# Gates as columns, spread by DMA, and merged products ahead of the short ones in a two-layer decoder trunk

## The chip, the core and the metric

The kernel runs on one core of one Trainium2 chip. A core has a matmul engine (TensorE, PE in the profile; its weight loads are PEld), a vector engine (VectorE, DVE), a scalar engine (ScalarE, ACT), a general engine (GpSimd, POOL) and an engine that only issues transfers (SyncE, SP). They work side by side and meet through semaphores. Transfers (DMAs) run on 16 DMA engines that all queues share; POOL, ACT and SP each have a queue for issuing them. The on-chip memory SBUF has 128 partitions; matmuls write to PSUM, eight banks of 512 floats per partition.

The metric is the device time of one execution, in microseconds, as the median over runs.

## The reference

256 tokens of width 1024 go through two layers. Each layer adds three branches to the running x: a SwiGLU feed-forward (hidden width 2816), an attention (block-sparse in layer 0, latent attention with a shared K/V in layer 1) and a second feed-forward. All data are 32-bit floats.

Every branch is modulated by a condition vector c. From `silu(c) @ ada_w + ada_b` come, per branch, a shift, a scale and a gate, each 1024 wide:

```python
mods = c_act @ ada_w[layer] + ada_b[layer]
sh1, sc1, g1, sh2, sc2, g2, sh3, sc3, g3 = jnp.split(mods, 9, axis=-1)
h = modulate(rms_norm(x, norm_g[layer, 0]), sh1, sc1)
x = x + 0.5 * g1[:, None, :] * swiglu(h, w_gate, w_up, w_down)
```

There are six gates (three branches in each of two layers). A gate multiplies the branch's output column by column, so all 256 rows see the same 1024 numbers. Shift and scale act on the normalised x in the same way.

## The kernel before

**Layout.** The 256 tokens are two tiles of 128. A branch's input h is held transposed (width on partitions, tokens along the row), so shift and scale are one number per partition there: a column. The branch's output has tokens on partitions and width along the row, so a gate has to be a row of 1024 numbers repeated on all 128 partitions: the tile `gate`.

**Products at full precision from rounded parts.** A weight tile is split by `split` (L643, L644) into a high part (a rounded copy on ACT) and a low part (what is left, on DVE); activations likewise. A product of two floats is high x high, high x low and low x high, accumulated in PSUM. In attention and in the down projection `mm3` (L773 to L775) issues these three, each over up to 512 columns. In the gate-and-up part of a feed-forward the weight is the stationary side, and the activations' high and low parts lie side by side (2 x 256 columns). There one *merged* product (L970, 512 columns) multiplies the weight's high part by both, and one *short* product (L977, 256 columns) multiplies the weight's low part by the activations' high part. The short one adds to the second half of the merged one's PSUM bank; ACT (L981) and DVE (L982) then sum the halves, L984 and L985 make `silu(gate) * up`, and L788 and L789 split the result for the down projection.

**The feed-forward's loops.** A block is 256 columns of the hidden width, with two weight tiles of 1 MB (one of w_gate, one of w_up), each split in two pieces of 1024 columns. It holds two steps of 128 hidden columns. In a step there are two parts, first "gate", then "up", and for each part the source issues eight merged products (over the 1024 input rows), then eight short ones, and then the evacuation of its PSUM bank. There are 35 blocks: 8 in the first feed-forward, 9 in each of the others, whose first 512 columns go through `mm3`. Then come the down projection, the residual (`resid`, L883, which multiplies by `gate`) and the next branch's norm, whose reciprocal root is a power on POOL (L810). The heads' norms in attention use POOL as well (L1138).

**The modulation vectors.** Their weights are streamed as 160 tiles of 512 KB. For shift and scale the weights are stored transposed: one DVE instruction (`column`, L654) multiplies a tile by the condition, which `c_b` repeats on all partitions, and sums along the row, which gives one column of 128 numbers, bias included. The read of its accumulator stands as a second small record on the same line. For a gate the weights are stored as they come: `ada_gate` adds eight tiles, each times the condition's column `cact`, into `acc` (L692, on DVE). POOL has filled `acc` with zeros (L690) and loaded the bias into its row 0 (L691). The sum over `acc`'s 128 partitions is still to be made: `acc` is split (a high part on ACT, a low part on DVE), two products by a matrix of ones (L702, L703) for each half of 512 columns sum it and repeat the sum on all partitions at once, in a PSUM buffer with a name of its own (`adaps`), and ACT copies it to `gate` with the factor 0.5 or 1 (L705).

**What sets the order.** The source is written against a rough clock of PE's work (`pe(us)`, `later(us, fn)`): `ada_pace` spreads the modulation tiles over a stage, `later` puts a piece of work behind so much PE work. After that the class `Order` plans anew: it takes all instructions with their dependences, an estimated duration for each (`duration`) and the buffer rings of every pool, and places them engine by engine, POOL's queue of transfers included; what it decides is written down as the fixed order of each engine. On PE it prefers, among what is ready, the instruction that comes first in the source; products into `adaps` go ahead of all others, or wait up to 3 us for their turn. On the other engines it takes the one that is needed soonest. The tiles of the last gate, (1, 2), are held until the last feed-forward has begun (`late`).

**Buffers that the change touches.** `ps_mm` has four PSUM banks for products (`mm_tile`), `ps_tr` three for transposes and scores (`tr_tile`), `ps_ada` one. `modp` has two gate tiles. `rawp` has three weight tiles, `splitp` eight high and eight low pieces.

Of the kernel before, what the change touches and what calls it, by code (L numbers as in the profile page):

```python
# [21 lines left out]
P = 128  # L22
D = 1024
# [47 lines left out]
NORMS = [(0, 0), (0, 1), (0, 2), (1, 0), (1, 1), (1, 2), "kv"]  # L71
NK = KD * len(NORMS)


# [52 lines left out]
def lay_out(v):  # L127
# [12 lines left out]
    out["first"] = out["first"].reshape(KD, P, 3, -1).transpose(0, 2, 1, 3)  # L140
    mats, cols, rows = [], np.zeros((P, 3, NK), np.float32), []
    for key, i in vectors():
        w, b, c = ((v["kv_ada_w"], v["kv_ada_b"], i) if key == "kv" else
                   (v["ada_w"][key[0]], v["ada_b"][key[0]], 3 * key[1] + i))
        w, b = w[:, c * D:(c + 1) * D], b[c * D:(c + 1) * D]
        mats.append((w if i == 2 else w.T).reshape(KD, P, D))
        if i == 2:
            rows.append(b)
        else:
            c0 = NORMS.index(key) * KD  # L150
            cols[:, i, c0:c0 + KD] = b.reshape(KD, P).T
    gains = np.concatenate([v["norm_g"].reshape(6 * KD, P), v["kv_norm_g"].reshape(KD, P)])
    cols[:, 2] = gains.T
    pos = np.ascontiguousarray(v["positions"].reshape(S))
    more = [v["c"].reshape(KD, P).T, pos.view(np.float32).reshape(NT, P).T]
    for n in ("moba_q_g", "moba_k_g"):
        more.append(np.tile(v[n][0], 2)[:, None])
    for g in (v["mla_q_g"][0], v["mla_k_g"]):
        more += [np.concatenate([g[:DH], np.ones(P - DH, np.float32)])[:, None], np.tile(g[None, DH:], (P, 1))]
    out.update(ada=np.stack(mats), rows=np.stack(rows), cols=np.concatenate([cols.reshape(P, -1), *more], axis=1))  # L160

# [376 lines left out]
def trunk(ctx: ExitStack, tc: tile.TileContext, a: dict, out: bass.AP):  # L538
# [88 lines left out]

    all_cols = cp.tile([P, 3 * NK + KD + NT + 4 + 2 * RO], F32, name="cols")
    places = {}
    c0 = 3 * NK  # L630
    for name, n in (("c", KD), ("pos", NT), ("moba_q", 1), ("moba_k", 1), ("q", 1), ("q_pe", RO), ("k", 1), ("k_pe", RO)):
        places[name] = all_cols[:, c0:c0 + n]
        c0 += n
    cols, cact = all_cols[:, :3 * NK].rearrange("p (i c) -> p i c", i=3), places["c"]
    m_cols = cp.tile([P, 2, NK], F32, name="m_cols")

# [36 lines left out]
    def ada_cols(j, key, i):  # L673
# [8 lines left out]
        yield  # L682

    def ada_gate(j, key, row):

        for k in range(KD):
            with noted(late if key == (1, 2) else set()):
                if k == 0:
                    acc = adap.tile([P, D], F32, tag="acc", name=nm("acc"), bufs=1)
                    nc.gpsimd.memset(acc, 0.0)  # L690
                    nc.gpsimd.dma_start(acc[0:1, :], a["rows"][row:row + 1, :])  # L691
                nc.vector.scalar_tensor_tensor(acc, ada_tile(j, k), cact[:, k:k + 1], acc, op0=ALU.mult, op1=ALU.add)  # L692
            if k < KD - 1:
                yield
        ahi, alo = split(acc, D)
        t = mods[key, "g"] = modp.tile([P, D], F32, tag="gate", name=nm("gate"))

        def sums():
            for hh in range(2):
                pt = ps_ada.tile([P, 512], F32, tag="ada", name=nm("adaps"))  # L700
                sl = slice(hh * 512, (hh + 1) * 512)
                nc.tensor.matmul(pt, ones_r, ahi[:, sl], start=True, stop=False)  # L702
                nc.tensor.matmul(pt, ones_r, alo[:, sl], start=False, stop=True)  # L703
                pe(0.44)
                nc.scalar.activation(t[:, sl], pt, AF.Copy, scale=1.0 if key[1] == 1 else 0.5)  # L705
            ready.add((key, "g"))
        later(3.0, sums)
        yield
# [185 lines left out]
    def ffn(layer, idx, h, after, ada_to, start=None):  # L894

        last = (layer, idx) == (1, 1)
        with ExitStack() as st:
# [50 lines left out]
            for f0 in range(B1 * P if start else FB, F, S):  # L948
# [9 lines left out]
                for f in range(f0 // P, (f0 + S) // P):  # L958
                    j = (f - f0 // P) % n
                    if not j:  # L960
                        both = (tp.tile([P, 512], F32, tag="ry", name=nm("ry"), bufs=1) if start else
                                sumsp.tile([P, 1024], F32, tag="both", name=nm("both")))
                        both = both.rearrange("p (i n t q) -> p i n t q", i=2, t=NT, q=P)
                    for i, pl in enumerate(parts):
                        ps = mm_tile()
                        for k in range(KD):
                            if len(pl) <= k:
                                pl += nextw()
                            wh = pl[k][0][:, f * P - f0:(f + 1) * P - f0]
                            nc.tensor.matmul(ps, wh, hk_both(h, k).rearrange("p i t q -> p (i t q)"),  # L970
                                             start=k == 0, stop=False)
                            pe(0.227)
                            if start and k in HOOKS and f0 < SIDE_TO * S:
                                bias_step()
                        for k in range(KD):
                            wl = pl[k][1][:, f * P - f0:(f + 1) * P - f0]
                            nc.tensor.matmul(ps[:, S:], wl, hk_both(h, k)[:, 0].rearrange("p t q -> p (t q)"),  # L977
                                             start=False, stop=k == KD - 1)
                            pe(0.12)
# [536 lines left out]
    def first(units):  # L1516
# [5 lines left out]
        with ExitStack() as st:  # L1522
# [30 lines left out]
            with ranked(0):  # L1553
                nc.scalar.activation(c_b[0:1, :], c_b[0:1, :], AF.Silu)
                for i in range(2):
# [3 lines left out]
                    nc.scalar.activation(c_b[:, half], pt, AF.Copy)  # L1559
                nc.scalar.activation(cact, cact, AF.Silu)  # L1560
            ps_x = [tr_tile(), ps_ada.tile([P, 512], F32, tag="ada", name=nm("tr"))]
# [113 lines left out]
```

## Time and profile before

| | us |
|---|---|
| median of three runs | 996.17 |
| lowest and highest run | 995.87, 996.71 |
| the profiled execution | 995.87 |
| its span, from first to last instruction | 994.1 |
| PE busy | 979.9 (99%) |
| DVE busy | 844.2 (85%) |
| ACT busy | 615.5 (62%) |
| POOL busy | 77.7 (8%) |

The profile's page gives the busy time of each engine, the costliest groups of instructions, and a chain of waits followed back from the last instruction. A row of a group reads: source line, engine, operation, what it writes and reads, count, then busy time in us, mean ns of one, and the idle time of the engine before them with what ended it. A row of the timeline or of the chain reads: start, duration, what. Matmuls are pipelined: the record of one with 512 columns lasts 0.39 us, while the next starts before it ends, so the cost of one is read from the distance of starts.

The stages lie as follows, by the timeline: the first feed-forward to about 208 us, the block-sparse attention to 330, the second feed-forward to 520, the third to 700, the latent attention to 805, the last feed-forward to the end.

### The profile page before, as it was taken

To read this page: it belongs to the slowest core of one execution; us is meant where nothing else is said; L and a number is where in the kernel's file an instruction comes from. 1 tells how busy PE (TensorE), PEld (TensorE's weight loads), DVE (VectorE), ACT (ScalarE), POOL (GpSimd) and SP (SyncE) were. 2 spreads that over 40 slices of the span, in tenths; PEclk is the share of its full clock that TensorE was granted. 3 is DMA by queue.
4 is the path that set the end of the run, shared out by engine and by line. 5 is a ranking of instruction groups with operands and counts; after the bars stand their busy time and mean duration, and the time that the engine had idled before them with its cause. 6 is when DMAs were issued, how large, how long until landed. Compare 5 with 4: busy or idle time off the path is not lost.

```text
span 994.1 us, 15134 instructions
## 1 busy us (share of the span) xinstructions
PE 979.9 (99%) x5558; PEld 831.1 (84%) x5558; DVE 844.2 (85%) x1391; ACT 615.5 (62%) x1113; POOL 77.7 (8%) x120
## 2 busy tenths in 40 slices
PE   9999999999999999999999999999989999999998
PEld 6988888878887888888888888888878888888886
DVE  7999999799999999999799999844998789667542
ACT  5689665378756965555377555643879685557421
POOL 2011000022221000000000000000052010000000
PEclk9999999999999999999999999999999999999999
DMA  9979889798887789988888999552343467444630
GB/s 353 403 289 304 333 292 358 299 339 333 284 313 246 267 326 330 326 299 310 340 332 330 340 320 327 208 195 88 106 154 128 170 253 287 180 170 175 227 127 21
DMA packets 54235, 260.51 MB, mean 262 GB/s; under 512 B 6289, under 2 KB 6801, under 8 KB 35986
## 3 DMA queue, kind: packets, MB, share of 16 engines
q1 hardware_dynamic: 52850, 256.06, 70.4%
q0 software_dynamic: 1024, 3.17, 1.1%
q8 instruction: 43, 0.70, 0.3%
q10 hardware_dynamic: 288, 0.33, 0.1%
q14 instruction: 30, 0.25, 0.1%
HBM read 255.34 MB, written 4.19 MB: 261 GB/s over the span
## 4 chain that ended last, share of the span: by engine, by line
PE 73%; DVE 10%; issue 10%; DMA 4%; ACT 2%; POOL 1%; SPq 0%; DVEq 0%; ACTq 0%; POOLq 0%
PE mm L970 21%; PE mm L773 12%; PE mm L775 12%; PE mm L774 12%; PE mm L977 11%; DVE lo L644 3%; DMA raw<-in_w_dram 2%; PE at L1101 1%; PE at L1078 1%; DMA adaw<-in_ada_dram 1%; PE tr L823 1%; DVE oh L1221 1%; DMA raw<-in_first_dram 1%; ACT hi L643 1%; DVE acc L692 1%
## 5 line engine op out<-in xcount | busy, mean ns | idle before, releaser
L644 DVE TENSOR_TENSOR lo<-raw,hi 128x1024 fp32r<-128x1024 f32 (+3 forms) x312 | 371.3, 1202 | 90.1 <-ACT hi L643 69.6
L643 ACT ACTIVATE hi<-raw 128x1024 fp32r<-128x1024 f32 (+3 forms) x312 | 315.8, 1038 | 157.9 <-PE mm L775 115.8
L970 PE MATMUL mm<-h,hi 128*128 128x512 f32 x1120 | 288.7, 394 | 0.8 <-ACT hi L643 0.8
L970 PEld LDWEIGHTS mm<-h,hi 128*128 128x128 f32 x1120 | 199.8, 189 | 36.0 <-ACT hi L643 1.0
L977 PEld LDWEIGHTS mm<-h,lo 128*128 128x128 f32 x1120 | 155.2, 190 | 11.9
L977 PE MATMUL mm<-h,lo 128*128 128x256 f32 x1120 | 162.1, 283 | 0.0
L654 DVE CUSTOM_DVE_ANT_0 adaw<-adaw,c_b,cols 128x1024 f32<-128x1024 f32 x112 | 141.8, 1279 | 1.9 <-DMA adaw<-in_ada_dram 1.9
L773 PE MATMUL mm<-hi,gh 128*128 128x512 f32 x352 | 137.3, 390 | 0.0
L775 PE MATMUL mm<-hi,gl 128*128 128x512 f32 x352 | 137.1, 389 | 0.0
L774 PE MATMUL mm<-lo,gh 128*128 128x512 f32 x352 | 137.0, 389 | 0.0
L981 ACT ACTIVATE both<-mm 128x256 f32<-128x256 f32 x108 | 40.5, 376 | 90.2 <-PE mm L977 89.8
L773 PE MATMUL mm<-hi,h 128*128 128x512 f32 (+1 forms) x240 | 94.5, 400 | 0.5 <-ACT h L788 0.5
L775 PE MATMUL mm<-hi,h 128*128 128x512 f32 (+1 forms) x240 | 92.4, 391 | 1.4 <-DVE h L789 1.4
L774 PE MATMUL mm<-lo,h 128*128 128x512 f32 (+1 forms) x240 | 93.3, 393 | 0.0
L775 PEld LDWEIGHTS mm<-hi,gl 128*128 128x128 f32 x352 | 66.1, 188 | 13.7
L774 PEld LDWEIGHTS mm<-lo,gh 128*128 128x128 f32 x352 | 66.1, 188 | 13.5
L773 PEld LDWEIGHTS mm<-hi,gh 128*128 128x128 f32 x352 | 66.1, 188 | 13.4
L692 DVE SCALAR_TENSOR_TENSOR acc<-adaw,cols,acc 128x1024 f32<-128x1024 f32 x48 | 61.5, 1282 | 0.1
L982 DVE TENSOR_TENSOR both<-both,mm 128x256 f32<-128x256 f32 x108 | 44.9, 416 | 12.0 <-ACT both L981 11.6
L775 PEld LDWEIGHTS mm<-hi,h 128*128 128x128 f32 x240 | 45.0, 188 | 10.3 <-DVE h L789 1.7
L773 PEld LDWEIGHTS mm<-hi,h 128*128 128x128 f32 x240 | 45.1, 188 | 10.1 <-issue 1.2
L774 PEld LDWEIGHTS mm<-lo,h 128*128 128x128 f32 x240 | 45.1, 188 | 7.7
(234 smaller groups left out, 1173.8 us busy)
## 6 DMA issues: line engine op xcount, KB each, us to landing
raw<-in_w_dram SPq DMA_DIRECT2D x142, 1024.0 KB, 6.0
adaw<-in_ada_dram SPq DMA_DIRECT2D x160, 512.0 KB, 5.7
raw<-in_first_dram SPq DMA_DIRECT2D x24, 256.0 KB, 7.5
raw<-in_w_dram SPq DMA_DIRECT2D x12, 512.0 KB, 3.6
raw<-in_w_dram SPq DMA_DIRECT2D x6, 576.0 KB, 3.7
bias_d<-bt SPq DMA_DIRECT2D x12, 256.0 KB, 5.8
bg<-bias_d POOLq DMA_DIRECT2D x4, 768.0 KB, 8.2
raw<-in_w_dram SPq DMA_DIRECT2D x2, 768.0 KB, 4.1
```

The source lines that it names most:

```text
L643: nc.scalar.activation(hi, src, AF.Copy)
L644: nc.vector.tensor_tensor(lo, src, hi.bitcast(F32), op=ALU.subtract)
L654: nc.vector.tensor_tensor_reduce(wt, wt, c_b, 1.0, cols[:, i, c:c + 1], op0=ALU.mult, op1=ALU.add, accum_out=m_cols[:, i, c:c + 1])
L692: nc.vector.scalar_tensor_tensor(acc, ada_tile(j, k), cact[:, k:k + 1], acc, op0=ALU.mult, op1=ALU.add)
L773: nc.tensor.matmul(ps, lh, rh, start=start, stop=False)
L774: nc.tensor.matmul(ps, lh, rl, start=False, stop=False)
L775: nc.tensor.matmul(ps, ll, rh, start=False, stop=stop)
L823: nc.tensor.transpose(kslice(pt, j), kslice(y, j), ident)
L970: nc.tensor.matmul(ps, wh, hk_both(h, k).rearrange("p i t q -> p (i t q)"), start=k == 0, stop=False)
L977: nc.tensor.matmul(ps[:, S:], wl, hk_both(h, k)[:, 0].rearrange("p t q -> p (t q)"), start=False, stop=k == KD - 1)
L981: nc.scalar.activation(sums, ps[:, S:], AF.Copy)
L982: nc.vector.tensor_tensor(sums, sums, ps[:, :S], op=ALU.add)
```

## The change

Two parts.

**Gates.** The weights of the gates are now stored transposed as well. `ada_gate` makes a gate like a shift: one multiply-and-sum on DVE per tile gives a column of 128 numbers with the bias, eight columns per gate, in `g_cols`. PE transposes the 128x8 columns to 8x128 in one of the `tr` banks, ACT copies them (factor 0.5 or 1) to `g_row`, POOL's queue stores these 4 KB in a tile in HBM, `gate_d`, and a second transfer on POOL's queue reads them back as one row of 1024 numbers, repeated on all 128 partitions, into `gate`. `acc` with its fill, its bias load, its split, the products by ones and the evictions of `adaps` go, and so do the condition as a column (`cact`) and its SiLU at the start. The biases of the gates travel in the packed columns.

**The feed-forward's order.** In a step, the merged products of "gate" and of "up" come first, then the short ones of "gate" with its evacuation, then the short ones of "up" with its evacuation. Both PSUM banks of the step are asked for ahead of the products.

```diff
-        mats.append((w if i == 2 else w.T).reshape(KD, P, D))
+        mats.append(w.T.reshape(KD, P, D))
         if i == 2:
-            rows.append(b)
+            gates.append(b.reshape(KD, P).T)
...
-    more = [v["c"].reshape(KD, P).T, pos.view(np.float32).reshape(NT, P).T]
+    more = [*gates, pos.view(np.float32).reshape(NT, P).T]
...
-    all_cols = cp.tile([P, 3 * NK + KD + NT + 4 + 2 * RO], F32, name="cols")
+    all_cols = cp.tile([P, 3 * NK + NGATE * KD + NT + 4 + 2 * RO], F32, name="cols")
...
+    gate_d = dp.tile([NGATE, KD, P], F32, name="gate_d")
+    g_cols = cp.tile([P, NGATE, KD], F32, name="g_cols")
+
     def ada_gate(j, key, row):
 
         for k in range(KD):
             with noted(late if key == (1, 2) else set()):
-                if k == 0:
-                    acc = adap.tile([P, D], F32, tag="acc", name=nm("acc"), bufs=1)
-                    nc.gpsimd.memset(acc, 0.0)
-                    nc.gpsimd.dma_start(acc[0:1, :], a["rows"][row:row + 1, :])
-                nc.vector.scalar_tensor_tensor(acc, ada_tile(j, k), cact[:, k:k + 1], acc, op0=ALU.mult, op1=ALU.add)
+                wt, c = ada_tile(j, k), row * KD + k
+                nc.vector.tensor_tensor_reduce(wt, wt, c_b, 1.0, places["gates"][:, c:c + 1], op0=ALU.mult, op1=ALU.add,
+                                               accum_out=g_cols[:, row, k:k + 1])
             if k < KD - 1:
                 yield
-        ahi, alo = split(acc, D)
         t = mods[key, "g"] = modp.tile([P, D], F32, tag="gate", name=nm("gate"))
 
-        def sums():
-            for hh in range(2):
-                pt = ps_ada.tile([P, 512], F32, tag="ada", name=nm("adaps"))
-                sl = slice(hh * 512, (hh + 1) * 512)
-                nc.tensor.matmul(pt, ones_r, ahi[:, sl], start=True, stop=False)
-                nc.tensor.matmul(pt, ones_r, alo[:, sl], start=False, stop=True)
-                pe(0.44)
-                nc.scalar.activation(t[:, sl], pt, AF.Copy, scale=1.0 if key[1] == 1 else 0.5)
+        def spread():
+            pt = tr_tile()
+            nc.tensor.transpose(pt[:KD, :P], g_cols[:, row], ident)
+            pe(0.11)
+            g_row = sp.tile([KD, P], F32, tag="grow", name=nm("grow"), bufs=1)
+            nc.scalar.activation(g_row, pt[:KD, :P], AF.Copy, scale=1.0 if key[1] == 1 else 0.5)
+            nc.gpsimd.dma_start(gate_d[row], g_row)
+            nc.gpsimd.dma_start(t, bcast_row(gate_d[row], D))
             ready.add((key, "g"))
-        later(3.0, sums)
+        later(3.0, spread)
...
-                    for i, pl in enumerate(parts):
-                        ps = mm_tile()
+                    pss = [mm_tile() for _ in parts]
+                    for ps, pl in zip(pss, parts):
                         for k in range(KD):
                             if len(pl) <= k:
                                 pl += nextw()
...
+                    for i, (ps, pl) in enumerate(zip(pss, parts)):
                         for k in range(KD):
                             wl = pl[k][1][:, f * P - f0:(f + 1) * P - f0]
                             nc.tensor.matmul(ps[:, S:], wl, hk_both(h, k)[:, 0].rearrange("p t q -> p (t q)"),
...
-                nc.scalar.activation(cact, cact, AF.Silu)
```

More of the change, by code (lines that the diff above doesn't have):

```diff
@@ L72 @@
 NK = KD * len(NORMS)
+NGATE = len(NORMS) - 1
 def vectors():
@@ L140, in lay_out @@
     out["first"] = out["first"].reshape(KD, P, 3, -1).transpose(0, 2, 1, 3)
-    mats, cols, rows = [], np.zeros((P, 3, NK), np.float32), []
+    mats, cols, gates = [], np.zeros((P, 3, NK), np.float32), []
     for key, i in vectors():
@@ L159, in lay_out @@
         more += [np.concatenate([g[:DH], np.ones(P - DH, np.float32)])[:, None], np.tile(g[None, DH:], (P, 1))]
-    out.update(ada=np.stack(mats), rows=np.stack(rows), cols=np.concatenate([cols.reshape(P, -1), *more], axis=1))
+    out.update(ada=np.stack(mats), cols=np.concatenate([cols.reshape(P, -1), *more], axis=1))
     table = np.concatenate([np.zeros((1, H), np.float32), v["rel_bias"]])
@@ L626, in trunk @@
     pos_f = a["positions"].rearrange("o s -> (o s)")
-    all_cols = cp.tile([P, 3 * NK + KD + NT + 4 + 2 * RO], F32, name="cols")
+    all_cols = cp.tile([P, 3 * NK + NGATE * KD + NT + 4 + 2 * RO], F32, name="cols")
     places = {}
     c0 = 3 * NK
-    for name, n in (("c", KD), ("pos", NT), ("moba_q", 1), ("moba_k", 1), ("q", 1), ("q_pe", RO), ("k", 1), ("k_pe", RO)):
+    for name, n in (("gates", NGATE * KD), ("pos", NT), ("moba_q", 1), ("moba_k", 1), ("q", 1), ("q_pe", RO), ("k", 1), ("k_pe", RO)):
         places[name] = all_cols[:, c0:c0 + n]
         c0 += n
-    cols, cact = all_cols[:, :3 * NK].rearrange("p (i c) -> p i c", i=3), places["c"]
+    cols = all_cols[:, :3 * NK].rearrange("p (i c) -> p i c", i=3)
     m_cols = cp.tile([P, 2, NK], F32, name="m_cols")
```

## The prediction, made before the changed kernel was run

> **What bounds the kernel now.** I read the page first: busy shares, then the chain of work that ended last.
>
> ```profile
> span 994.1 us, 15134 instructions
> ...
> PE 979.9 (99%) x5558; PEld 831.1 (84%) x5558; DVE 844.2 (85%) x1391; ACT 615.5 (62%) x1113; POOL 77.7 (8%) x120
> ...
> PE 73%; DVE 10%; issue 10%; DMA 4%; ACT 2%; POOL 1%; SPq 0%; DVEq 0%; ACTq 0%; POOLq 0%
> ```
>
> The matmul engine is busy 99% of the span and carries 73% of the chain. A busy PE could still be a slow one, so I next read busy times by stage (columns: PE, weight loads, DVE, ACT, POOL, then clock, DMA share, GB/s).
>
> ```profile
> 50.00:90.00 40.00, 39.23 (x461) 33.34 (x460) 39.87 (x102) 37.06 (x82) 6.35 (x37) 1.00 0.82 292
> 90.00:152.00 62.00, 61.97 (x351) 54.04 (x351) 61.21 (x110) 41.15 (x75) 4.32 (x5) 1.00 0.88 315
> 208.00:330.00 122.00, 121.51 (x682) 97.56 (x681) 115.88 (x224) 89.26 (x189) 26.24 (x17) 1.00 0.82 294
> 352.00:454.00 102.00, 102.00 (x585) 89.46 (x584) 98.06 (x136) 61.41 (x95) 2.98 (x4) 1.00 0.90 324
> 695.00:805.00 110.00, 104.96 (x657) 89.33 (x656) 96.43 (x225) 87.36 (x220) 26.24 (x25) 1.00 0.40 137
> ```
>
> In the gate-and-up part of a feed-forward (352 to 454) PE has no gap at all; in the first one (50 to 152) DVE is just as full (39.87 of 40.00, 61.21 of 62.00). The last question is what one matmul costs in the stream. The chain of waits inside that part, and a row from each end of a steady run of 512-column products (20 starts, 199.79 to 204.09), give it:
>
> ```profile
> 376.94 0.95 PE mm L977 x8
> 377.89 1.84 PE mm L970 x8
> ```
> ```profile
> 199.79 0.39 PE L773 MATMUL mm<-hi,gh 128*128 128x512 f32 x1
> ...
> 204.09 0.39 PE L774 MATMUL mm<-lo,gh 128*128 128x512 f32 x1
> ```
>
> A merged product (512 columns) costs 1.84 / 8 = 0.230 us, a short one (256 columns) 0.95 / 8 = 0.119 us, whatever the 0.39 us that a record lasts. So PE sets the end, and a matmul taken out of its queue is worth its 0.23 us wherever PE has no gap around it.
>
> **The gates: what goes.** Per gate four products over 512 columns of ones leave PE, with two evictions and a split on ACT, a split on DVE, and a fill and a small load on Pool.
>
> ```profile
> L654 DVE CUSTOM_DVE_ANT_0 adaw<-adaw,c_b,cols 128x1024 f32<-128x1024 f32 x112 | 141.8, 1279 | 1.9 <-DMA adaw<-in_ada_dram 1.9
> ...
> L692 DVE SCALAR_TENSOR_TENSOR acc<-adaw,cols,acc 128x1024 f32<-128x1024 f32 x48 | 61.5, 1282 | 0.1
> ...
> L654 DVE DVE_READ_ACCUMULATOR2_ANT m_cols<- 128x1 f32 x112 | 9.2, 82 | 0.0
> ...
> L644 DVE TENSOR_TENSOR lo<-acc,hi 128x1024 fp32r<-128x1024 f32 x6 | 7.3, 1224 | 1.9 <-PE mm L977 1.8
> L705 ACT ACTIVATE gate<-adaps 128x512 f32<-128x512 f32 x12 | 7.1, 594 | 2.4 <-PE adaps L703 2.2
> ...
> L643 ACT ACTIVATE hi<-acc 128x1024 fp32r<-128x1024 f32 x6 | 6.4, 1062 | 2.6 <-PE mm L970 1.6 <-PE mm L775 1.0
> ...
> L702 PE MATMUL adaps<-hi,ones_r 128*128 128x512 f32 x12 | 4.8, 401 | 0.0
> ...
> L703 PE MATMUL adaps<-lo,ones_r 128*128 128x512 f32 x12 | 4.7, 396 | 0.0
> ```
>
> PE: 12 products at L702 and 12 at L703, 24 x 0.230 = 5.5 us less, all on the path. ACT loses 6.4 + 7.1 = 13.5 us and DVE 7.3 us of splits; both are cover, priced at nothing of their own since PE has no gap there to close. The 48 products of a weight tile with the condition stay on DVE under another instruction, 1.279 us against 1.282 us: no change. (Its accumulator read adds at most 48 x 0.082 = 3.9 us to DVE, less than the 7.3 us that go.) Six fills and six loads leave Pool, which is 8% busy.
>
> **The gates: what comes.** Per gate one transpose on PE, a small copy on ACT (the 128x512 eviction takes 0.59 us; an 8x128 one not more), and on Pool's queue a 4 KB store and a 512 KB load that spreads the row. The trace has transposes in the stream of products only in pairs:
>
> ```profile
> 212.01 0.38 PE L823 MATMUL tr<-ident,y 128*128 128x128 f32 x2
> 212.15 0.48 PE L773 MATMUL mm<-hi,h 128*128 128x512 f32 x1
> 212.46 0.39 PE L773 MATMUL mm<-hi,gh 128*128 128x512 f32 x1
> ```
>
> From 212.01 to 212.46 pass 0.45 us for a pair and one product; less 0.23, a pair costs 0.22 us. A single one costs between 0.11 (half) and 0.22 (if the switch, not the second tile, is the price); I take 0.12, since a second transpose only adds its own stream. Six: 0.7 us, at most 1.3. (Each now borrows one of the three transpose buffers for its copy instead of a buffer of its own; at most 0.59 us six times, and the third buffer covers it.) The gates' sum on PE is -5.5 + 0.7 = -4.8 us, -4.2 at the dear end.
>
> The two transfers follow one another, since the second reads what the first stored. Their nearest rows are the small loads on the same queue and the bias loads (768 KB):
>
> ```profile
> L691 POOL DMA_DIRECT2D acc<-in_rows_dram x6: 501/547/669, 2.5 to 799.6; - x6
> ...
> DMA to landing us min/median/max: 1.7/3.6/5.7
> ```
> ```profile
> bg<-bias_d POOLq DMA_DIRECT2D x4, 768.0 KB, 8.2
> ```
>
> By the medians a gate is 3.6 + 8.2 = 12 us later than its transpose, by the worst store 5.7 + 8.2 = 14 us. The tightest gate is the first: its last eviction starts at 133.60, and the residual that reads it at 182.55.
>
> ```profile
> 133.60 0.60 ACT L705 ACTIVATE gate<-adaps 128x512 f32<-128x512 f32 x1
> ```
> ```profile
> 182.55 0.68 DVE L883 TENSOR_TENSOR ry<-mm,gate 128x512 f32<-128x512 f32 x1
> ```
>
> That is 48 us of cover for 14, so the latency costs nothing; without cover it would be 14 us a gate. The page DMA: Bandwidth & Descriptors of the Trainium skill (section "Anatomy of one DMA") gives 2.0 us plus bytes over 436 GB/s per transfer on this path, as an estimate 2.0 + 3.2 = 5.2 us for the two; by either the cover holds.
>
> ```profile
> cols<-in_cols_dram SPq DMA_DIRECT2D x1, 123.0 KB, 2.2
> ```
>
> At the start, one SiLU of eight columns on ACT goes, and the packed columns grow by 40 floats a partition (3 x 56 + 48 + 70 = 286 for 246); 20 KB beside weights at 292 GB/s and more is 0.07 us. I count neither.
>
> **The feed-forward's order.** The 35 blocks hold 140 runs of eight merged products and 140 of eight short ones; afterwards two runs of a kind follow each other, so about 70 changes of length each way go. Eight steady 512-column products cost 8 x (204.09 - 199.79) / 19 = 1.81 us; after short ones eight cost 1.84. So a change costs 0.03 us, of which the short side gives some 0.01 back: 70 x 0.02 = 1.4 us, between 0 (if the 0.03 belongs to the operands' places, not to the change) and 2.1. I take 1.2.
>
> The second half of each pair ("up") is wanted 0.95 us earlier in its split's high part, and the low part of "gate" 1.84 us later. Where the high part is late, PE waits. One such wait stands at the first block:
>
> ```profile
> 51.34 2.00 PE L970 MATMUL mm<-h,hi 128*128 128x512 f32 x8
> 53.18 1.11 PE L977 MATMUL mm<-h,lo 128*128 128x256 f32 x8
> 55.06 1.20 PE L970 MATMUL mm<-h,hi 128*128 128x512 f32 x4 [0.77 <-ACT hi L643]
> ```
> ```profile
> L970 PE MATMUL mm<-h,hi 128*128 128x512 f32 x1120 | 288.7, 394 | 0.8 <-ACT hi L643 0.8
> ```
>
> There the short products would follow instead of precede, and the block ends when it did. The group of all 1120 merged products has 0.8 us of idle time, which is this one, so elsewhere the splits run ahead. The two accumulators of a pair are held together, but the four PSUM buffers turn over in two pairs of 5.58 us (2 x 2.79), and an evacuation needs about 1: no wait. The evacuations move with the short products: that of "gate" comes 1.84 us later, just ahead of that of "up", and what follows (sum, SiLU, split) still has the next pair's 5.58 us.
>
> **Sum.** -4.8 - 1.2 = -6.0 us. The profiled execution took 995.87 us around its span of 994.1; 995.87 - 6.0 = 989.9, and against the median of 996.17, 990.2 us. Its own bounds: -4.2 - 0 gives 992.0, and -4.8 - 2.1 gives 989.3.
>
> **Rivals.**
> *Gates alone.* The source only proposes PE's order; the planner in the kernel places each instruction, and may interleave the runs anyway. Then -4.8: 991.4. Against it: in the rows at 376.94 its order is the source's.
> *More than the sum.* Net of the accumulator reads DVE loses some 3.5 us, most of it in stages where it is full. If all of that closes gaps of PE (994.1 - 979.9 = 14.2 us of them), 986.7. The full stages hold little of them (40 - 39.23, 122 - 121.51), so little supports it.
> *Given back.* The new plan makes "up" wait for its high split. If one block of six loses 0.95 us, 35 / 6 x 0.95 = 5.5 us return: 995.7. For it: DVE and ACT orders are planned anew everywhere; against: the 0.8 us of idle time above.
> *Pool's queue held.* The spreading load waits on Pool for the store to land, and what stands behind it there waits too. At the change from feed-forward to attention this is the norm's power:
>
> ```profile
> 208.06 1.47 POOL L810 TENSOR_TENSOR rstd<-ssq,mhalf 128x1 f32<-128x1 f32 x1 [85.09 <-DVE ssq L805]
> ...
> 215.91 1.07 POOL L1253 DMA_DIRECT2D bg<-bias_d  x1 [4.64 <-PE mm L775]
> 219.57 1.47 POOL L810 TENSOR_TENSOR rstd<-ssq,mhalf 128x1 f32<-128x1 f32 x1 [2.60 <-DVE ssq L805]
> ```
>
> A second gate transposed near 207 and a load issued just ahead of 219.57 cost 0.55 + 5.7 + 1.07 = 7.3 us at worst: 990.2 + 7.3 = 997.5. Against: the planner holds the load back until it reckons the store landed, and 11 us lie between the two powers. The page SBUF — State Buffer of the Trainium skill (section "Who interferes with whom") warns that DVE copies in their two-port mode lock Pool out while it writes descriptors, some 0.6 us becoming 3.1; the L691 row, 0.50 to 0.67 us beside a DVE at 85%, does not show it.
> *Slower: the spreading loads push the weights.* Six times 512 KB at 315 GB/s are 6 x 1.67 = 10.0 us of transfer time in stages whose DMA share is 0.82 to 0.90. If the weights have no reserve, PE waits all of it: 990.2 + 10.0 = 1000.2. The sign turns where a load holds PE up by 1.0 us. The waits speak against it:
>
> ```profile
> ACT hi L643 <- PE mm L775: 116.8, 77, 9.1
> ...
> ACT hi L643 <- DMA raw<-in_w_dram: 9.2, 7, 1.9
> ```
>
> The splits wait for buffers that PE frees (116.8 us), seldom for weights (9.2).
>
> **How the numbers follow.** Forecast 0.50, gates alone 0.16, more than the sum 0.08, given back 0.12, Pool's queue 0.06, weights pushed 0.08. A measurement of this kernel tells about 0.2% (2 us) from no change: the first three are faster (0.74), given back and Pool's queue same (0.18), the last slower (0.08). The range 987.0 to 996.5 leaves out the last two and part of "more".
>
> **What would show it.** No L702 and L703, six transposes, DVE's lo<-acc gone; merged products in runs of 16 near 3.65 us and short ones near 1.91; the spreading loads landing within 14 us, tens of us ahead of L883; idle time of the merged products still near 1 us. Wrong would make it: that idle time at several us, the norm's power late with a load ahead of it, or splits waiting on weights for clearly more than 9.2 us.

## The result, and the profile after

The changed kernel takes 990.18 us (median of six runs, 989.76 to 990.75); the kernel before, run beside it, 996.02 (995.33 to 996.76). The ratio is 0.9938, with an interval of 0.9927 to 0.9949: 5.8 us faster, where 990.2 was predicted. The profiled execution took 989.81 us.

The first lines of the page, and its chain by engine, of the changed kernel:

```profile
span 988.0 us, 15123 instructions
...
PE 975.1 (99%) x5540; PEld 829.4 (84%) x5540; DVE 834.3 (84%) x1433; ACT 606.0 (61%) x1100; POOL 76.9 (8%) x120
...
PE 89%; DVE 6%; DMA 2%; ACT 1%; issue 1%; POOL 0%; SPq 0%; DVEq 0%; ACTq 0%
```

The span is 6.1 us shorter, PE is as full as before, and PE now carries 89% of the chain. DVE is busy for 9.9 us less and ACT for 9.5.

The chain of waits inside the second feed-forward of the changed kernel (start, us, what) shows the new order of products:

```profile
376.84 1.91 PE mm L979 x16
378.76 3.65 PE mm L971 x16
382.41 1.91 PE mm L979 x16
```

Sixteen merged products take 3.65 us, sixteen short ones 1.91. Before, the same 32 products took 2 x (1.84 + 0.95) = 5.58 us, now 5.56. That is 0.02 us for the one change of length each way that went. Over all undisturbed steps of the two traces the medians are 5.587 and 5.567 us, so the 0.02 is not a matter of rounding.

A gate's transpose among merged products, by the timeline of PE in the changed kernel:

```profile
356.21 0.86 PE L971 MATMUL mm<-h,hi 128*128 128x512 f32 x3
356.91 0.27 PE L701 MATMUL tr<-ident,g_cols 128*8 128x128 f32 x1
356.94 1.39 PE L971 MATMUL mm<-h,hi 128*128 128x512 f32 x5
```

The next product starts 0.03 us after the transpose. Its group of five lasts 1.39 us, of which the last product's record is 0.39: 1.00 us from the first start to the fifth, where four steady distances are 4 x 0.227 = 0.91. So the transpose costs 0.03 + 0.09 = 0.12 us, paid by the product behind it. By the starts, all six transposes of the trace come out at 0.11 to 0.12 us.

The groups by line in the changed kernel (busy us, mean ns | idle before):

```profile
L971 PE MATMUL mm<-h,hi 128*128 128x512 f32 x1120 | 270.3, 392 | 0.6 <-ACT hi L644 0.6
...
L693 DVE CUSTOM_DVE_ANT_0 adaw<-adaw,c_b,cols 128x1024 f32<-128x1024 f32 x48 | 60.7, 1276 | 0.0
...
L693 DVE DVE_READ_ACCUMULATOR2_ANT g_cols<- 128x1 f32 x48 | 3.8, 80 | 0.0
```

No new idle time stands before the merged products: 0.6 us, against 0.8.

The two transfers of a gate, by the landings of lines L705 and L706 of the changed kernel (4 KB store, then the 512 KB spread), and the first reading of a spread gate on DVE:

```profile
L705 POOL DMA_DIRECT2D gate_d<-grow x6: 522/570/697, 128.1 to 894.6; - x6
...
DMA to landing us min/median/max: 4.1/4.7/5.5
```
```profile
L706 POOL DMA_DIRECT2D gate<-gate_d x6: 546/561/587, 133.0 to 899.6; - x6
...
DMA to landing us min/median/max: 3.6/6.3/9.4
```
```profile
182.68 0.69 DVE L884 TENSOR_TENSOR ry<-mm,gate 128x512 f32<-128x512 f32 x1
```

The first spread is issued at 133.0, lands by 143 at the latest, and is read at 182.68: 40 us of reserve. From the issue of the store to the landing of the spread the six gates take 8.5 to 14.3 us.

POOL's timeline where the second gate meets the norms, in the changed kernel:

```profile
205.71 1.47 POOL L811 TENSOR_TENSOR rstd<-ssq,mhalf 128x1 f32<-128x1 f32 x1 [72.09 <-DVE ssq L806]
208.98 0.57 POOL L705 DMA_DIRECT2D gate_d<-grow  x1 [1.79 <-ACT grow L704]
213.17 1.08 POOL L1255 DMA_DIRECT2D bg<-bias_d  x1 [3.63 <-PE tr L824]
214.24 0.55 POOL L706 DMA_DIRECT2D gate<-gate_d  x1
216.98 1.48 POOL L811 TENSOR_TENSOR rstd<-ssq,mhalf 128x1 f32<-128x1 f32 x1 [2.19 <-DVE ssq L806]
```

The store lands at 213.71, the spread goes out 0.5 us later behind a bias load, and the norm's second power waits for DVE, not for the queue. At the other five gates POOL stands still for 4 to 5 us between store and spread, with no norm near.

### The profile page after: what moved, and what is told of

Read it like the earlier page. It is cut to its first block, busy times and chain, and to the rows that moved or that the text cites. A ratio compares the mean times of both kernels' runs of the same rounds, so it can differ in the third digit from the quotient of the medians.

```text
span 988.0 us, 15123 instructions
## 1 busy us (share of the span) xinstructions
PE 975.1 (99%) x5540; PEld 829.4 (84%) x5540; DVE 834.3 (84%) x1433; ACT 606.0 (61%) x1100; POOL 76.9 (8%) x120
## 3 DMA queue, kind: packets, MB, share of 16 engines
q0 software_dynamic: 1888, 6.32, 1.9%
## 4 chain that ended last, share of the span: by engine, by line
PE 89%; DVE 6%; DMA 2%; ACT 1%; issue 1%; POOL 0%; SPq 0%; DVEq 0%; ACTq 0%
PE mm L971 26%; PE mm L774 14%; PE mm L775 14%; PE mm L776 14%; PE mm L979 14%; DMA raw<-in_first_dram 2%; PE at L1103 1%; DVE lo L645 1%; PE at L1080 1%; PE tr L1204 1%; PE at L1033 1%; DVE adaw L655 1%; PE at L1041 1%; DMA adaw<-in_ada_dram 1%; PE tr L824 1%
## 5 line engine op out<-in xcount | busy, mean ns | idle before, releaser
L971 PE MATMUL mm<-h,hi 128*128 128x512 f32 x1120 | 270.3, 392 | 0.6 <-ACT hi L644 0.6
L971 PEld LDWEIGHTS mm<-h,hi 128*128 128x128 f32 x1120 | 205.3, 188 | 40.5 <-ACT hi L644 0.8
L979 PEld LDWEIGHTS mm<-h,lo 128*128 128x128 f32 x1120 | 144.5, 191 | 5.7
L979 PE MATMUL mm<-h,lo 128*128 128x256 f32 x1120 | 147.7, 283 | 0.0
L655 DVE CUSTOM_DVE_ANT_0 adaw<-adaw,c_b,cols 128x1024 f32<-128x1024 f32 x112 | 141.4, 1277 | 0.7 <-DMA adaw<-in_ada_dram 0.7
L693 DVE CUSTOM_DVE_ANT_0 adaw<-adaw,c_b,cols 128x1024 f32<-128x1024 f32 x48 | 60.7, 1276 | 0.0
```

Of the source, the lines that this page charges most:

```text
L655: nc.vector.tensor_tensor_reduce(wt, wt, c_b, 1.0, cols[:, i, c:c + 1], op0=ALU.mult, op1=ALU.add, accum_out=m_cols[:, i, c:c + 1])
L693: nc.vector.tensor_tensor_reduce(wt, wt, c_b, 1.0, places["gates"][:, c:c + 1], op0=ALU.mult, op1=ALU.add, accum_out=g_cols[:, row, k:k + 1])
```

## Where each part's time lies

The change has two parts, so most of the runs split it. For a comparison by place I gave every matmul a nominal length (0.227 us for 512 columns, 0.120 for 256, and so on; the gates' sums, the masks and the fillers nothing), added these up in the order of the starts, and read for each trace at what time it had the same sum behind it. The table gives the gain (-) or loss (+) against the kernel before in each stretch, in us; the stretches are named by their times in the kernel before. It rests on one profiled execution of each kernel, so a transfer that happened to be late in that execution stands in it too (two such cases are named below), and work that a plan moves across a border shows up on both sides of it.

| kernel | 0-60 start | 60-280 first feed-forward, two gates | 280-345 end of first attention | 345-500 second feed-forward, two gates | 500-700 third feed-forward, one gate | 700-800 latent attention | 800-end fourth feed-forward, one gate | span |
|---|---|---|---|---|---|---|---|---|
| terms of the prediction | 0 | -1.9 | 0 | -1.9 | -1.1 | 0 | -1.1 | -6.0 |
| changed | +0.1 | -2.4 | +1.2 | -2.0 | -1.2 | -0.7 | -1.2 | -6.1 |
| changed, pairs kept | 0.0 | -2.0 | +1.1 | -2.1 | -1.1 | -0.5 | -1.1 | -5.7 |
| changed, second plan | +0.3 | -2.1 | +1.9 | -2.0 | -1.1 | -0.6 | -1.1 | -4.8 |
| changed, splits put back | -0.3 | -1.4 | +1.6 | -2.0 | -1.2 | -0.6 | -1.1 | -5.0 |
| changed, loads four times | +0.2 | -2.6 | +1.2 | -2.0 | -1.2 | -0.6 | -1.1 | -6.1 |
| gates alone | +0.6 | -2.3 | +2.5 | -1.7 | -0.8 | -0.5 | -0.5 | -2.7 |
| gates alone, second plan | +0.5 | -2.2 | +2.5 | -1.7 | -0.5 | -0.4 | -0.8 | -2.6 |
| order alone | +0.7 | +0.8 | 0.0 | -0.3 | -0.3 | -0.3 | -0.3 | +0.3 |
| order alone, second plan | +0.2 | +0.5 | +1.7 | -0.2 | -0.3 | -0.5 | -0.2 | +1.1 |
| order with DVE's relief | +0.2 | -0.2 | +2.1 | -0.3 | -0.2 | -0.5 | -0.3 | +0.8 |
| gates, runs of four | +0.4 | -1.9 | +2.5 | -1.5 | -0.4 | -0.5 | -0.4 | -1.6 |
| gates, runs of thirty-two | +0.6 | 0.0 | +1.6 | -2.2 | -0.6 | -0.6 | 0.0 | -1.3 |
| before, second plan | -0.1 | -0.3 | +1.3 | +0.1 | -0.1 | -0.4 | +0.1 | +0.6 |

In the second, third and fourth feed-forward the terms stand nearly as predicted (0.3 us for the order, 0.8 for a gate), and there the two parts add up within 0.3 us. At the start, in the first feed-forward and at the end of the first attention they don't. The experiments below are about these.

## Experiments

Each ratio is taken against runs of the kernel before that were made beside it. Their median is 996.33 us for the gates alone, the order alone and the runs of four and of thirty-two; 996.38 for the second plans of the changed kernel and of the kernel before, the pairs kept together and the splits put back; 996.04 for the rest.

**Gates alone.** The changed kernel with the feed-forward's source order as before:

```diff
-                    pss = [mm_tile() for _ in parts]
-                    for ps, pl in zip(pss, parts):
+                    for i, pl in enumerate(parts):
+                        ps = mm_tile()
...
-                    for i, (ps, pl) in enumerate(zip(pss, parts)):
```

> The changed gates with the old order of the feed-forward. Theory (the two parts add up: 24 products of 0.230 us go from PE, six transposes of some 0.12 us come; the order is worth 1.2 us of changes of length): 991.4 us, 1.2 above the changed kernel and 4.6 to 4.8 below the kernel before. Rival, the order is worth nothing (the 0.03 us at the head of a run belong to the operands' places): 990.2, like the changed kernel. Rival, the gain is mostly the order's, by waits that it removes: 993 or more.

Measured 993.22 us, ratio 0.9968 (0.9955 to 0.9980): 3.1 us of the expected 4.8.

**Order alone.** The opposite edit, on the kernel before.

> The old gates with the new order of the feed-forward. Theory: 1.2 us below the kernel before, 994.8 us against 996.0, from 70 changes of length each way that go. Rival, the order is worth nothing: 996.0. Rival, the order removes waits too or is what carries the gain: 993 or less.

Measured 996.78 us, ratio 1.0006 (0.9997 to 1.0014): nothing of the expected 1.2. So the parts bring 3.1 and nothing alone, and 5.8 together. In the first feed-forward this trace has a wait that the kernel before lacks. PE's and DVE's timeline of the kernel with the order alone:

```profile
124.00 0.73 PE L970 MATMUL mm<-h,hi 128*128 128x512 f32 x2 [1.14 <-DVE ry L983]
```
```profile
122.39 1.23 DVE L644 TENSOR_TENSOR lo<-acc,hi 128x1024 fp32r<-128x1024 f32 x1
123.53 0.42 DVE L983 TENSOR_TENSOR ry<-ry,mm 128x256 f32<-128x256 f32 x1
```

The merged product waits 1.14 us for an evacuation (`ry`), because its PSUM bank is still full; and right ahead of that evacuation on DVE stands `lo<-acc`, the split of a gate, one of the six that the gates' part takes away. So it looks as if the parts depended on each other here; the runs on DVE's relief below test that, and bear it out in part at most.

**Runs of four and of thirty-two.** The changed gates, with four merged and four short products in turn, and with the merged products of both steps of a block ahead of all its short ones:

```diff
...
+                        for k0 in range(0, KD, 4):
+                            for k in range(k0, k0 + 4):
...
+                            for k in range(k0, k0 + 4):
...
```
```diff
+                fs = range(f0 // P, (f0 + S) // P)
+                pss = {}
+                for f in fs:
+                    pss[f] = [mm_tile() for _ in parts]
...
+                for f in fs:
```

> The changed gates, and in the feed-forward runs of four merged and four short products in turn: 280 changes of length each way, where the changed kernel has 70. Theory (each change costs PE 0.014 to 0.02 us; with four products the slow start is not quite over, so the low end): 3.0 us above the changed kernel, 993.2. Rival, the slow start belongs to the first five of the eight weight places and not to the change of length: 990.2, since every place is visited as often.

> The changed gates, and in the feed-forward all 32 merged products of a block first, then its 32 short ones, which holds all four PSUM buffers of products: 35 changes each way. Theory: 0.6 us below the changed kernel, 989.6, since the first buffer has 2.9 us for its evacuation before the next block wants it. Rival, the buffers bind: the next block waits for an evacuation, 0.5 to 1 us in each of 35 blocks, 1007 or more.

Measured 993.90 us (ratio 0.9976, 0.9967 to 0.9985) and 994.01 (0.9974, 0.9965 to 0.9983). Against the gates alone, runs of four are 0.7 us slower; against the changed kernel 3.7, where 3.0 was expected, but by the table 1.3 of these 3.7 stand at the end of the first attention, where no run length was changed. The price of a change can be read from the steps that nothing interrupts. From start to start, 32 products take 5.613 us in runs of four, 5.587 in runs of eight, 5.567 in runs of sixteen and 5.557 in runs of thirty-two (medians over all such steps of these traces). Between eight and thirty-two a change of length each way costs 0.020 us, between four and eight 0.013: so a change has no fixed price. The rival, by which the slow start belongs to the weight places, would have left all four alike. The 140 more changes of the runs of four would make 1.8 us at 0.013, if no step were interrupted; in the last three feed-forwards the merged and short products alone took 0.24, 0.44 and 0.38 us longer than in the gates alone. In runs of thirty-two all four banks are taken before the first evacuation. That pays in the second feed-forward (-2.2 for -2.0 us), and in the first one the merged products wait for DVE's evacuations, by PE's timeline of this kernel:

```profile
97.89 3.92 PE L968 MATMUL mm<-h,hi 128*128 128x512 f32 x16 [1.30 <-DVE ry L987]
...
102.97 1.21 PE L968 MATMUL mm<-h,hi 128*128 128x512 f32 x4 [0.57 <-DVE ry L987]
```

By the table the third and the fourth feed-forward lose 0.6 and 1.2 us against the changed kernel. The 1.2 are not PE's: from the start of the last product to the end of the span this execution took 6.32 us, those of the other kernels 5.12 to 5.35, and the store of the last result makes the difference. The cause of the 0.6 was not followed up. Neither of the two times expected of this kernel came.

**A second plan of the same work.** To learn what a new plan alone does, I changed the margin with which the planner chooses, in the changed kernel and in the kernel before. No work is added or taken:

```diff
-MARGIN = 400.0
+MARGIN = 420.0
```

> The changed kernel with the planner's margin at 420 for 400: no work is added or taken, about 100 lines of PE's order stand elsewhere. Theory of scatter: between 988.5 and 992.0 us, off 990.2 by 0.5 us or more. Rival, the work alone sets the time: 990.2 us within 0.3.

> The kernel before with the planner's margin at 420 for 400: no work is added or taken, about 350 lines of PE's order stand elsewhere, and the pair of score products of the last head group is split as in the changed kernels. Theory of scatter: between 996.5 and 998.5 us, above the kernel before by the 1 to 2 us that the kernels with changed gates lose at that place. Rival, the work alone sets the time: 996.2 us within 0.3.

Measured 991.22 us (0.9949, 0.9936 to 0.9963) for the changed kernel, 1.0 us above its first plan, and 997.26 (1.0010, 1.0001 to 1.0019) for the kernel before, 0.9 us above its own. The intervals leave little beside zero (those of the two plans of the changed kernel overlap), but the traces show where another plan of the same work differs: most of it lies at the end of the first attention. The group of score products there, of the kernel before, of its second plan and of the changed kernel:

```profile
L1039 PE MATMUL at<-kT,qT 64*128 64x256 f32 x32 | 4.1, 376 | 0.0
```
```profile
L1039 PE MATMUL at<-kT,qT 64*128 64x256 f32 x32 | 5.2, 380 | 0.0
```
```profile
L1041 PE MATMUL at<-kT,qT 64*128 64x256 f32 x32 | 5.3, 380 | 0.0
```

The same 32 products, and 1.1 to 1.2 us more. The timeline of PE shows the piece, first of the kernel before, then of the changed one:

```profile
307.89 1.58 PE L1039 MATMUL at<-kT,qT 64*128 64x128 f32 x16
309.40 0.50 PE L774 MATMUL mm<-lo,oT 128*128 128x512 f32 x1
```
```profile
304.83 1.58 PE L1041 MATMUL at<-kT,qT 64*128 64x128 f32 x12
306.35 0.73 PE L774 MATMUL mm<-hi,oT 128*128 128x512 f32 x2
307.01 1.13 PE L1041 MATMUL at<-kT,qT 64*128 64x256 f32 x4
308.06 0.50 PE L775 MATMUL mm<-lo,oT 128*128 128x512 f32 x1
```

Before, sixteen products of 64 rows go through in 309.40 - 307.89 = 1.51 us. In the changed kernel they go as twelve and four, in 1.52 and 1.05 us: 1.06 us more. These products come in pairs that use different halves of the array's rows, and the plan has torn the last four from their partners, so that all eight with 256 columns run alone: their starts lie 0.22 us apart, where before two of a pair start 0.007 us apart and the next pair 0.21 us later. The Trainium skill says under "Part 3: Packing small matmuls — row/col tiling" of TensorE: Matmul & The Clock Gate that products in different row groups run concurrently; the rows agree, 0.26 us for each of the four alone (the step to the next product included), and 1.51 / 16 = 0.09 in the piece of pairs (which holds shorter products too). Of all the traces only those of the kernel before and of the order alone have the 4.1 us. The kernel before was measured with a good draw at this place, and the change was charged for it.

The gates alone have the same 1.2 us, and a second 1.2 in the products with the values, first of the kernel before, then of the gates alone (their second plan shows the same 14.3):

```profile
L1101 PE MATMUL at<-pT,v 128*64 128x128 f32 x192 | 13.1, 280 | 0.0
```
```profile
L1102 PE MATMUL at<-pT,v 128*64 128x128 f32 x192 | 14.3, 280 | 0.0
```

Together 2.4 us by busy time, 2.1 from start to start, of the 2.5 that the table has there.

**Pairs kept together.** The changed kernel, with one rule more for the planner, that of such a pair the second never goes first:

```diff
         for a, b in self.twin.items():
...
+            self.after[a].append(b)
+            self.npre[b] += 1
```

> The changed kernel, with one rule more for the planner: of two score products that the source issues as a pair (64 rows each, in different row groups), the second is never placed ahead of the first. Theory that the plan's scatter moves the time by a few us: in the changed kernel the last two head groups of the block-sparse attention run four score products one after another that run in pairs elsewhere; the sum of that line from start to start grew by 1.05 us against before. With the pairs together 990.2 - 1.0 = 989.2 us, down to 988.2 if the whole jump of 2 us that stands there goes with it. Rival, the parts explain all and the split pair costs nothing since another wait ends there as late: 990.2 us. Rival, the new plan scatters as much the other way: 991 to 992 us.

Measured 990.69 us (0.9940, 0.9928 to 0.9953): no gain. The line did recover, as the timeline and the group of this kernel show,

```profile
308.32 1.13 PE L1043 MATMUL at<-kT,qT 64*128 64x256 f32 x8
```
```profile
L1043 PE MATMUL at<-kT,qT 64*128 64x256 f32 x32 | 4.5, 402 | 0.0
```

eight products in the time that four took alone. But the stretch lost 1.1 us against before all the same. The new plan runs the score products of the last two head groups in four pieces, where the kernel before has two (3.42 for 3.02 us from start to start), and the products with the values in four for three (3.49 for 3.18); the rest is spread over many lines. A rule for one line doesn't take the scatter away.

**The splits put back.** The changed kernel, with a split per gate on ACT and DVE whose results nothing reads:

```diff
+        split(c_b, D)
```

> The changed kernel with a split of 128x1024 numbers put back per gate (one rounding on ACT of 1.06 us and one subtraction on DVE of 1.22 us, six of each), whose results nothing reads; PE does the work of the changed kernel. Theory that only PE's products count: 990.2 us, give or take the plan's scatter of 1 to 2 us. Rival, that DVE's and ACT's relief was part of the gain: 990.2 + 3.5 = 993.7 us, with the feed-forward stages longer by 0.5 us or more at each gate.

Measured 990.01 us (0.9938, 0.9925 to 0.9950): the same as the changed kernel. ACT's and DVE's relief is not where the gain comes from. The profiled execution, 990.86 us, has a wait of PE for an evacuation in the first feed-forward,

```profile
96.55 0.73 PE L972 MATMUL mm<-h,hi 128*128 128x512 f32 x2 [1.37 <-DVE ry L985]
```

where the changed kernel has none of 0.1 us. But that is not the splits': the first of them stands at 119.5 us on ACT and at 123.9 on DVE. What stands ahead of it is a weight tile that came late, for which ACT waits, first in this kernel, then in the changed one:

```profile
90.69 1.06 ACT L644 ACTIVATE hi<-raw 128x1024 fp32r<-128x1024 f32 x1 [3.38 <-DMA raw<-in_w_dram]
```
```profile
89.75 1.06 ACT L644 ACTIVATE hi<-raw 128x1024 fp32r<-128x1024 f32 x1 [0.95 <-DMA raw<-in_w_dram]
```

The split of that tile starts 0.94 us later, and so do DVE's evacuations behind it, while PE is 0.46 us ahead of the changed kernel: 1.40 together, for a wait of 1.37. At the gates, where the splits were put back, PE waits for no evacuation.

**The order with DVE's relief.** The order alone, with the low part of each gate left out: `acc` is not split, and the second product of each pair reads the high part again at half scale. The gates are thus rounded, and PE does the same products:

```diff
-        ahi, alo = split(acc, D)
+        ahi = splitp.tile([P, D], F32R, tag="hi", name=nm("hi"))
+        nc.scalar.activation(ahi, acc, AF.Copy)
...
-                nc.tensor.matmul(pt, ones_r, alo[:, sl], start=False, stop=True)
+                nc.tensor.matmul(pt, ones_r, ahi[:, sl], start=False, stop=True)
...
```

> The feed-forward order alone, on the old gates, with DVE's relief but none of PE's: the gate's low part is left out (six subtractions of 1.22 us on DVE), and the second product of each pair reads the high part again, at half scale, so that PE does the same products as before. Theory that the order needs DVE's relief: in the kernel with the order alone a merged product of the first feed-forward waits 1.1 us for DVE's evacuation; here that wait goes and the order gives its 1.2 us: 995.1 us, the stage's wait of merged products on DVE under 0.5 us. Rival, the order gives nothing by itself: 996.8 us as with the order alone.

Measured 996.83 us (1.0008, 0.9999 to 1.0016). The theory falls as put: the wait is halved but not gone, though no split of a gate stands ahead of it any more,

```profile
119.63 0.73 PE L971 MATMUL mm<-h,hi 128*128 128x512 f32 x2 [0.61 <-DVE ry L984]
```

and its plan loses 2.1 us at the end of the first attention, more than the order can give. With that loss taken off, 994.8 would be left, but this is arithmetic and not a run.

**Second plans of the halves.** The same margin of 420 in the kernel with the order alone and in that with the gates alone.

> The feed-forward order alone on the old gates, with the planner's margin at 420 for 400, a second plan of the same work. Theory of scatter by the plan: within 1.5 us of 996.8, and where the wait of the first feed-forward for DVE's evacuation stays (1.1 us), not under 996. Rival, the order costs nothing and gives 1.2 us in any plan: 995.0 us.

> The gates alone in the old feed-forward order, with the planner's margin at 420 for 400, a second plan of the same work. Theory that the gates give 4.8 us and a plan scatters by about 1 us: 991.4 us, between 990.4 and 993.2. Rival, the gates alone give only the 3.1 us of the first plan, the rest needs the order: 993.2 us within 0.3.

Measured 996.49 us (1.0006, 0.9998 to 1.0015) and 993.16 (0.9970, 0.9958 to 0.9981). For the order, theory as expected: the wait for the evacuation is there again, 0.67 us, with `lo<-acc` ahead of the evacuation once more. For the gates alone the rival's number came out, 993.2. That the second plan repeats the first means little, though, since it tears the same pieces at the same place (+2.5 in both).

**Loads four times.** The changed kernel, with the spreading load of four of the gates issued four times:

```diff
-            nc.gpsimd.dma_start(t, bcast_row(gate_d[row], D))
+            for _ in range(1 if row < 2 else 4):
+                nc.gpsimd.dma_start(t, bcast_row(gate_d[row], D))
```

> The changed kernel with the spreading load of the gates of rows 2 to 5 issued four times over, into the same tile: 12 loads of 512 KB more, 12 x 1.67 = 20.0 us of transfer time at 315 GB/s. PE does the work of the changed kernel. Theory that the weights have a reserve: 990.2 us, up to 992 by the plan's scatter, and the splits' wait on weights stays under 25 us. Rival, weights pushed: each load holds PE up by 1.67 us, 990.2 + 20.0 = 1010.2 us; by half of it 1000.2 us.

Measured 989.83 us (0.9939, 0.9925 to 0.9952). Its page's row of the loads, and its waits, beside the same waits of the changed kernel:

```profile
gate<-gate_d POOLq DMA_DIRECT2D x18, 512.0 KB, 7.7
```
```profile
ACT hi L644 <- PE mm L777: 97.7, 70, 9.1
POOL gate L707 <- DMA gate<-gate_d: 82.2, 12, 8.7
...
ACT hi L644 <- DMA raw<-in_w_dram: 23.3, 16, 4.5
```
```profile
ACT hi L644 <- PE mm L776: 112.9, 79, 9.1
...
ACT hi L644 <- DMA raw<-in_w_dram: 17.7, 14, 2.3
```

Twelve loads more keep POOL waiting for 82 us and cost PE nothing. ACT's waits on weights grow at the expense of its waits on PE's buffers. The weights have a reserve of at least 20 us of transfer time over these stages (six of the twelve loads lie in the second feed-forward, three each in the third and the fourth). The first feed-forward got no such load; there the trace of the splits put back has shown that a late weight tile does reach PE.

## Why the prediction was right

*What bounds the kernel* was right: every matmul taken out of PE's queue gave its steady cost, and ACT's and DVE's relief gave nothing that the median shows.

*The gates, -4.8.* In the kernel before, the 24 products took 5.67 us from start to start, 0.236 each where 0.230 was taken. The transposes cost 0.11 to 0.12 us each, the value chosen between 0.11 and 0.22. In the stretch 345-500, the gates alone gave 1.7 us for two gates, 0.85 each; the step put it at 0.8.

*The latency of the two transfers, nothing.* The medians are 4.7 + 6.3 = 11.0 us where 12 was worked out, the slowest gate 14.3 against 14; the cover of 40 us held. The 5.2 us estimated from the Trainium skill (DMA: Bandwidth & Descriptors, "Anatomy of one DMA") were less than half of it; beside DMA engines this busy the rows decide.

*The order, -1.2.* Sixteen and sixteen products took the 3.65 and 1.91 us that were named, and the order alone gave 0.2 to 0.3 us in each of the last three feed-forwards, 1.2 for four at the upper end. By the merged and short products alone it is 0.31 to 0.36 us in each of the three, on the old gates and on the new. But "no wait" does not hold in every plan. The step reckoned with the turnover of PSUM buffers and about 1 us for an evacuation; it left out what stands ahead of the evacuation on a DVE that is full in the first feed-forward. The order alone waits there 1.14 us in one plan and 0.67 in the other, the second plan of the changed kernel 0.3, the changed kernel itself under 0.1. That the gates' splits make this difference is not shown: without them half of the wait stayed, and with them put back none came at a gate.

*Work not touched, nothing.* This term was not in the sum at all, and it is the one that was wrong: the planner lays out everything anew. In the changed kernel it lost 1.2 us at the end of the first attention and gained 0.7 in the latent attention and 0.5 in the first feed-forward, by luck close to zero in all. Most of the gain in the latent attention is one shorter wait of PE for `s`, the exponentials on ACT. The rows are of the kernel before, of its second plan (which does the same work) and of the changed kernel:

```profile
743.70 0.97 PE L1473 MATMUL tr<-ident,qn 128*96 128x128 f32 x7 [1.41 <-ACT s L1063]
```
```profile
744.89 1.08 PE L1473 MATMUL tr<-ident,qn 128*96 128x128 f32 x8 [1.02 <-ACT s L1063]
```
```profile
738.54 1.08 PE L1475 MATMUL tr<-ident,qn 128*96 128x128 f32 x8 [0.52 <-ACT s L1065]
```

In the kernels with one part it didn't cancel. The time of 990.2 was therefore hit closer than the method allows; over the five plans of the changed kernel that were run (two of them with idle splits or loads added) the times are 989.8 to 991.2.

*The rivals.* Gates alone (991.4): the planner kept the source's order, by the rows at 376.84; that kernel itself took 993.2. More than the sum (986.7): refuted by the 990.2 itself and by the splits put back, 990.0. Given back (995.7): the merged products' wait for the high split stayed at 0.6 us. Pool's queue (997.5): refuted by POOL's timeline from 205.71 to 216.98. Issues of 0.52 to 0.70 us on POOL beside a DVE busy 84% show nothing of the lock that the Trainium skill describes (SBUF — State Buffer, "Who interferes with whom"). They are a weak test of it: the Trainium skill ties the full lock there to copies, casts and `tensor_scalar` in a two-port mode, and most of DVE's instructions here are `TENSOR_TENSOR` (818 in the changed kernel, beside 109 `TENSOR_SCALAR` and 9 casts). Weights pushed (1000.2): refuted by the loads issued four times over.

*What would show it.* One sign was badly chosen. ACT's wait on weights went from 9.2 to 17.7 us, which the prediction would have taken as a sign against itself. ACT has that time to spare: what it waits for weights it no longer waits for buffers, and PE's merged products still idle 0.6 us.

What stays open: why the planner tears the pairs in all plans but two (and the one with the rule), what moves the start by up to 0.7 us, and why the order alone waits for an evacuation in the first feed-forward where the changed kernel with the splits put back waits at no gate.

## What to carry to other kernels

Where one engine is full, price a change by the steady distance of starts of the instructions that it takes from that engine, and expect that where the stage has no other wait; what the freed helpers lose or gain is worth nothing until they stand ahead of something that engine needs. When a planner lays out the whole kernel anew, give untouched stages a scatter in the range (here about 1 us), and measure it with a second plan of the same work before a half of the change is judged by its own time. Two parts that were measured one by one need not add up: each time holds the scatter of its own plan, here as large as a part.

## What was not expected of the hardware

A product over few rows is cheap or dear by its neighbour: four score products of 64 rows and 256 columns without partners took 1.05 us, eight in pairs 1.07 (308.32, and the next product at 309.39). And the product behind a gate's transpose starts only 0.03 us after it; the rest of its cost shows up in that product's distance to the next (0.31 us instead of 0.23), so the transpose's own row (0.27 us) tells neither. A change of length in the stream of products costs 0.020 us each way in runs of eight and more, and 0.013 in runs of four.
